# Spreading the heads' norm roots on ScalarE, and moving two pairs of value heads out of PSUM in one operation

## The chip, the cores and the metric

The kernel runs on one core of a Trainium2 chip. The metric is the device time of one execution in microseconds (us). TensorE (PE) does the matmuls; its weight loads (PEld) are listed apart. VectorE is DVE, ScalarE is ACT, GpSimd is POOL, and SyncE (SP) issues most of the transfers.

## The reference, cut to what matters

Two layers over x of 512 tokens by 1024 features. A layer is a gated feed-forward block, a token mixer with three groups of heads, and a second feed-forward block. All of it is float32. The mixer, with what the change touches:

```python
proj = h @ w_in[layer]
(qa, ka, va, qb, kb, vb, qi, ki, wi, qc, kc, vc) = jnp.split(proj, split_points, axis=-1)
oa = moba_attention(qa, ka, heads(va, N_HEADS_A))                # 4 heads, softmax
ob = dsa_attention(qb, kb, heads(vb, N_HEADS_B), qi, ki, wi)     # 4 heads, softmax over 128 chosen keys
oc = stick_breaking_attention(heads(qc, N_HEADS_C), heads(kc, N_HEADS_C), heads(vc, N_HEADS_C))  # 8 heads
o = jnp.concatenate([oa, ob, oc], axis=2)
o = (_rms(o).reshape(B, S, D_MIX) * out_g[layer].astype(jnp.float32)).astype(x.dtype)
x = x + g2 * (o @ w_out[layer])
```

Each head has 64 features. `_rms` divides each head's output, token by token, by the root of its mean square over those 64 features.

## The kernel before, in words

Activations lie with features on the 128 partitions and the 512 tokens along the row. Each float32 product is made of three matmuls of a faster format: every operand is split into a high part (a cast, on ACT) and a low part (a subtraction, on DVE), and `mm3` multiplies high by high, high by low and low by high (L323 to L325). So every piece of weights costs a transfer into one of three `raw` buffers, a cast to `whi` (L285) and a subtraction to `wlo` (L295), with five buffers for each of the two.

Work in the mixer goes by pairs of heads, eight pairs in all (0 to 3 softmax, 4 to 7 stick-breaking). The steps of all the pairs are Python generators, and a string written out by hand, `PLAN`, says which generator is advanced next. It begins

```python
ki ki ki q0 ki q0 q0 ki ki q0 ki q0 q0 c4 q0 c4 q1 q0 q1 c4 ...
```

where `ki` is the projection of the indexer's keys together with the values of pairs 4 and 5, `q0` and `q1` are projections of the indexer's queries, `c4` is the projection of queries and keys of pair 4, and the `n` steps finish a pair. The framework below it plans each engine's queue when the program is built: it takes the instructions by their place in the program, but lets one that it reckons ready go ahead of an earlier one that it reckons is still waiting. It reckons with durations of its own. It also puts all waits in. On the chip each queue then runs strictly in the planned order. Where an instruction of ACT and one of DVE read the same PSUM tile, the framework lets one wait for the other.

Values leave PSUM in `put_v`: for one tile of 128 tokens and one pair of heads (128 columns), ACT casts the columns to the high half of the tile `v` (L672) and DVE subtracts to get the low half (L673). `v_pairs` and `index_k` project the values of two pairs at once, 256 columns of one PSUM bank, and call `put_v` for one pair and then for the other. Four token tiles for each of four such groups make 32 calls in a layer. In `index_k` the evacuation of a token tile is four casts or copies on ACT (keys to `tok` at L809, indexer weights to `wi` at L810, two values at L672) and two subtractions on DVE. After the last tile, `do_rope` turns part of the keys (L651 to L654), L830 copies them, and the PE transposes them (L660) into a bank of the tag `b`, of which there are two. The first rows of the PE's queue behind that are the third tile of `q0`.

A pair is finished in `finish_pair`: ACT squares the output (L700), the PE sums the squares of each head (L706) into a bank, and `rsqrt` works out the roots on a tile of 128 partitions by 8 (4 token tiles, 2 heads). In these steps `self.logs` is true: DVE forms the argument (L337, or L341 to L343 for softmax pairs), ACT takes a logarithm and an exponential (L348, L349), and DVE makes one Newton step (L355, L356, L358). Before, the last operation of this chain also spreads each root over the 64 features of its head, by reading the small tile with a repeated index and writing 512 columns into the tile `of`: for stick-breaking pairs that is L358 itself, for softmax pairs a multiplication by the reciprocal of the softmax sum (L363). The PE then transposes the spread tile (L717), and DVE multiplies the pair's output by it (L719). There are nine finishes in a layer: seven with 512 columns and, for pair 3, two halves with 256.

Of the kernel before, what the change touches and what calls it, by code (L numbers as in the profile page):

```python
# [19 lines left out]
F32R = mybir.dt.float32r  # L20
# [3 lines left out]
ALU = mybir.AluOpType  # L24
# [3 lines left out]
P = 128  # L28
S = 512
NT = S // P  # L30
# [7 lines left out]
HD = 64  # L38
# [5 lines left out]
NIH = 8  # L44
# [141 lines left out]
class Net:  # L186
# [140 lines left out]

    def rsqrt(self, ss, shape, inv, r=None, wide=None, pin=False):  # L330

        nc = self.nc
        mk = lambda tag: self.t(self.sp, "%s%d" % (tag, int(np.prod(shape[1:]))), shape, bufs=2)
        v, y, u = mk("rv"), mk("ry"), mk("ru")
        spread = lambda t: t if wide is None else t[:, :, :, None].to_broadcast(list(wide.shape))
        if r is None:
            first = nc.vector.tensor_scalar(v, ss, inv, EPS, op0=ALU.mult, op1=ALU.add)  # L337
            if pin:
                self.tc.keep_in_program_order(first)
        else:  # L340
            nc.vector.scalar_tensor_tensor(v, ss, inv, r, op0=ALU.mult, op1=ALU.mult)  # L341
            nc.vector.tensor_mul(v, v, r)
            nc.vector.tensor_scalar(v, v, EPS, None, op0=ALU.add)  # L343
        if shape[-1] == 2 and len(shape) == 2:
            self.rsqrt_done = nc.gpsimd.tensor_tensor(y, v, self.half.to_broadcast(shape), op=ALU.pow)
            return y
        if self.logs:
            nc.scalar.activation(u, v, AF.Ln)  # L348
            nc.scalar.activation(y, u, AF.Exp, scale=-0.5)  # L349
        else:  # L350
            nc.vector.tensor_scalar(y.bitcast(I32), v.bitcast(I32), -0.5, float(0x5F3759DF),
                                    op0=ALU.mult, op1=ALU.add)
        rounds = 1 if self.logs else 3
        for i in range(rounds):
            nc.vector.tensor_mul(u, y, y)  # L355
            nc.vector.scalar_tensor_tensor(u, u, -0.5, v, op0=ALU.mult, op1=ALU.mult)  # L356
            last = i == rounds - 1 and r is None
            done = nc.vector.scalar_tensor_tensor(wide if last and wide is not None else y,  # L358
                                                  spread(u) if last else u, 1.5, spread(y) if last else y,
                                                  op0=ALU.add, op1=ALU.mult)  # L360
        self.rsqrt_done = done
        if r is not None:
            nc.vector.tensor_mul(wide, spread(y), spread(r))  # L363
        return y


# [296 lines left out]

    def new_v(self):
        return self.t(self.mp, "v", [P, NT, 2, 2, HD], F32R, bufs=4)

    def put_v(self, v, t, ps):

# [24 lines left out]
    def finish_pair(self, l, pair, cs=slice(0, S)):  # L695

        nc = self.nc
        o = self.o[pair]
        sq = self.t(self.mp, "of", [P, S], bufs=2)
        nc.scalar.activation(sq[:, cs], o[:, cs], AF.Square)  # L700
        yield
        tiles = range(cs.start // P, cs.stop // P)
        n = len(tiles)
        ss = self.bank("b", [P, n, 2])
        for i, t in enumerate(tiles):
            nc.tensor.matmul(ss[:, i, :], sq[:, t * P:(t + 1) * P], self.bones, start=True, stop=True)  # L706
        yield
        r = None
        if pair < 4:
            r = self.t(self.sp, "rs", [P, n, 2], bufs=2)  # L710
            nc.vector.reciprocal(r, self.sums[pair][:, tiles[0]:tiles[0] + n, :])
        yb = sq[:, cs].rearrange("p (t e d) -> p t e d", e=2, d=HD)
        self.rsqrt(ss, [P, n, 2], 1.0 / HD, r, yb)
        yield
        f = self.bank("b", [P, S])
        for i, t in enumerate(tiles):
            nc.tensor.transpose(f[:, t * P:(t + 1) * P], yb[:, i].rearrange("p a b -> p (a b)"), self.ident)  # L717
        yield
        nc.vector.scalar_tensor_tensor(o[:, cs], o[:, cs], self.outg[:, l, pair:pair + 1], f[:, cs],  # L719
                                       op0=ALU.mult, op1=ALU.mult)  # L720
        yield
# [80 lines left out]
    def index_k(self, l):  # L802
        nc, mp = self.nc, self.mp
        ki = self.t(mp, "tok", [P, NT, 2, HD], bufs=2)
        self.wi = self.t(mp, "wi", [P, NT, NIH], bufs=1)
        self.v.update({j: self.new_v() for j in (4, 5)})

        def evac(t, ps):
            nc.scalar.copy(ki[:, t, 0, :], ps[:, 0:HD])  # L809
            nc.scalar.copy(self.wi[:, t, :], ps[:, HD:HD + NIH])  # L810
            for i, j in enumerate((4, 5)):
                c = HD + NIH + i * P
                self.put_v(self.v[j], t, ps[:, c:c + P])

        rng = MIX_GROUPS["kiv"]
        n = sum(b - a for a, b in rng)
# [113 lines left out]
            yield from put(self.qk[4 + j], ps, scale)  # L930

    def v_pairs(self, l, grp, chunks):
        vs = {j: self.new_v() for j in chunks}
        self.v.update(vs)
        yield from self.proj_tok(l, grp, range(NT), lambda t, ps: [
            self.put_v(vs[j], t, ps[:, i * P:(i + 1) * P]) for i, j in enumerate(chunks)])

    def unit(self, pair, u):
        if pair >= 4:
# [241 lines left out]
```

## Time and profile before

| | |
|---|---|
| median of three timed runs | 2131.05 us (2129.67 to 2131.19) |
| the profiled execution: its own time | 2131.03 us |
| its span in the profile | 2129.2 us |
| PE busy | 2093.3 us (98%), 11327 matmuls |
| weight loads busy | 1803.8 us (85%) |
| DVE busy | 1276.1 us (60%) |
| ACT busy | 837.5 us (39%) |
| mean granted clock of TensorE | 0.998 |

Times inside the profile count from the start of the span. The two mixers lie at about 394 to 700 us and 1448 to 1755 us; the rest is feed-forward. A number in square brackets at the end of a timeline row is the time for which the engine sat idle before that row, and behind the arrow stands what released it as far as the profile can tell: a wait for several things is put down to the one that came last by the profile. "x4" at the end of a row means that four like instructions in a row are merged. The clock column is the share of full speed that TensorE was granted.

### The profile page before, as it was taken

How to read it: one execution, taken by the hardware profiler on the slowest of the kernel's cores; microseconds unless marked ns; L12 is line 12 of the kernel's file. 1: busy time of each engine (PE TensorE's matmuls, PEld its weight loads, DVE VectorE, ACT ScalarE, POOL GpSimd, SP SyncE). 2: the span in 40 equal slices, each digit the busy share in tenths (PEclk: the TensorE clock that was granted, in tenths of full speed). 3: DMA queues.
4: the chain of work that ended last, by engine and by line, in shares of the span. 5: the costliest groups of instructions: out<-in, count | busy, mean ns of one | idle time of the engine just before them, and what ended most of it. 6: DMA issues, size and time to landing. Idle time of an engine off the chain costs nothing.

```text
span 2129.2 us, 28611 instructions
## 1 busy us (share of the span) xinstructions
PE 2093.3 (98%) x11327; PEld 1803.8 (85%) x11327; DVE 1276.1 (60%) x2325; ACT 837.5 (39%) x1347; POOL 10.8 (1%) x24
## 2 busy tenths in 40 slices
PE   9999999999999999999999999999999999999999
PEld 6888888888998888888898888888889988888888
DVE  8773753679978677375364333346899776333332
ACT  3322222467675522222243222324766644222220
POOL 0000000000000000000000000000000000000000
PEclk9999999999999999999999999999999999999999
DMA  7883852342333388386234333324334223333331
GB/s 300 274 277 99 274 167 89 104 116 63 98 94 99 116 273 271 98 278 196 89 109 130 98 99 99 92 83 123 91 87 105 72 73 109 98 91 99 99 100 59
DMA packets 86150, 281.75 MB, mean 132 GB/s; under 512 B 10752, under 2 KB 13312, under 8 KB 86016
## 3 DMA queue, kind: packets, MB, share of 16 engines
q1 hardware_dynamic: 84576, 277.83, 42.3%
q8 instruction: 89, 1.46, 0.3%
q10 hardware_dynamic: 1440, 2.10, 0.3%
q14 instruction: 45, 0.37, 0.1%
HBM read 256.55 MB, written 2.10 MB: 121 GB/s over the span
## 4 chain that ended last, share of the span: by engine, by line
PE 81%; DVE 11%; ACT 3%; DMA 2%; issue 2%; POOL 0%; SPq 0%; POOLq 0%; DVEq 0%; ACTq 0%
PE z L323 23%; PE z L325 22%; PE z L324 22%; PE b L323 3%; PE b L325 3%; PE b L324 3%; DVE sc L881 2%; DVE m L880 2%; DVE wlo L295 2%; DVE att L594 1%; PE z L639 1%; PE z L683 1%; DMA qk<-qk 1%; DMA adaw<-in_w_ada_dram 1%; DVE tf L744 1%
## 5 line engine op out<-in xcount | busy, mean ns | idle before, releaser
L295 DVE TENSOR_TENSOR wlo<-raw,whi 128x1024 fp32r<-128x1024 f32 (+1 forms) x338 | 412.2, 1220 | 535.7 <-ACT whi L285 534.0
L285 ACT CAST whi<-raw 128x1024 fp32r<-128x1024 f32 (+1 forms) x338 | 354.9, 1050 | 842.0 <-PE z L324 772.4
L323 PE MATMUL z<-hh,whi 128*128 128x512 f32 (+1 forms) x1616 | 595.0, 369 | 3.0 <-ACT hh L454 2.3
L324 PE MATMUL z<-hl,whi 128*128 128x512 f32 (+1 forms) x1616 | 595.4, 369 | 0.3
L325 PE MATMUL z<-hh,wlo 128*128 128x512 f32 (+1 forms) x1616 | 594.5, 369 | 1.0 <-DVE wlo L295 1.0
L323 PEld LDWEIGHTS z<-hh,whi 128*128 128x128 f32 x1616 | 304.6, 189 | 55.4 <-ACT hh L454 3.9
L325 PEld LDWEIGHTS z<-hh,wlo 128*128 128x128 f32 x1616 | 304.8, 189 | 52.7 <-DVE wlo L295 2.1
L324 PEld LDWEIGHTS z<-hl,whi 128*128 128x128 f32 x1616 | 305.0, 189 | 51.5 <-DVE hl L455 1.2
L323 PE MATMUL z<-gh,whi 128*128 128x512 f32 (+1 forms) x792 | 290.9, 367 | 0.5 <-DVE xs L531 0.5
L324 PE MATMUL z<-gl,whi 128*128 128x512 f32 (+1 forms) x792 | 289.5, 366 | 0.0
L325 PE MATMUL z<-gh,wlo 128*128 128x512 f32 (+1 forms) x792 | 286.1, 366 | 0.0
L374 DVE CUSTOM_DVE_ANT_0 adaw<-adaw,silc 128x1024 f32<-128x1024 f32 x144 | 171.0, 1221 | 32.5 <-DMA adaw<-in_w_ada_dram 32.5
L323 PEld LDWEIGHTS z<-gh,whi 128*128 128x128 f32 x792 | 149.3, 188 | 28.0 <-DVE xs L531 1.2
L325 PEld LDWEIGHTS z<-gh,wlo 128*128 128x128 f32 x792 | 149.3, 189 | 24.6
L324 PEld LDWEIGHTS z<-gl,whi 128*128 128x128 f32 x792 | 149.4, 189 | 23.4
L323 PE MATMUL b<-whi,hh 128*128 128x256 f32 x544 | 156.9, 288 | 3.0 <-DVE v L673 2.1
L325 PE MATMUL b<-whi,hl 128*128 128x256 f32 x544 | 154.9, 285 | 0.0
L324 PE MATMUL b<-wlo,hh 128*128 128x256 f32 x544 | 154.8, 285 | 0.0
L531 DVE SCALAR_TENSOR_TENSOR xs<-z,mod,xs 128x512 f32<-128x512 f32 (+1 forms) x72 | 49.8, 691 | 120.8 <-PE z L325 120.8
L323 PEld LDWEIGHTS b<-whi,hh 128*128 128x128 f32 x544 | 105.1, 193 | 4.1 <-DVE osb L719 1.3
L324 PEld LDWEIGHTS b<-wlo,hh 128*128 128x128 f32 x544 | 105.0, 193 | 0.2
L325 PEld LDWEIGHTS b<-whi,hl 128*128 128x128 f32 x544 | 104.9, 193 | 0.0
(151 smaller groups left out, 2244.4 us busy)
## 6 DMA issues: line engine op xcount, KB each, us to landing
raw<-in_w_dram SPq DMA_DIRECT2D x332, 512.0 KB, 3.6
adaw<-in_w_ada_dram SPq DMA_DIRECT2D x144, 512.0 KB, 4.9
qk<-qk SPq DMA_DIRECT2D x144, 128.0 KB, 2.4
qk<-qk SPq DMA_DIRECT2D x24, 96.0 KB, 2.7
xs<-in_x_dram SPq DMA_DIRECT2D x4, 512.0 KB, 5.1
raw<-in_w_dram SPq DMA_DIRECT2D x4, 492.0 KB, 3.7
silc<-in_c_dram SPq DMA_DIRECT2D x3, 512.0 KB, 6.7
out_dram<-xs ACTq DMA_DIRECT2D x6, 256.0 KB, 2.0
```

Source lines behind the costliest of these rows:

```text
L285: nc.scalar.copy(hi[:, :n], raw[:, :n])
L295: self.nc.vector.tensor_sub(lo[:, :n], raw[:, :n], hi.bitcast(F32)[:, :n])
L323: mm(out, l[0], r[0], start=start, stop=False, **kw)
L324: mm(out, l[0], r[1], start=False, stop=False, **kw)
L325: mm(out, l[1], r[0], start=False, stop=stop, **kw)
L374: r = self.nc.vector.tensor_tensor_reduce(w, w, self.silc, 1.0, 0.0, op0=ALU.mult, op1=ALU.add, accum_out=m[:, j:j + 1])
L531: nc.vector.scalar_tensor_tensor(self.x[m][:, cs], ps[:, cs], gate[:, m:m + 1], self.x[m][:, cs], op0=ALU.mult, op1=ALU.add)
L594: nc.vector.tensor_sub(unit_sbuf(lo, u), src, unit_sbuf(hi.bitcast(F32), u))
L639: self.nc.tensor.matmul(out, a, b, start=start and i == 0, stop=stop and i == 1, skip_group_check=True)
L683: nc.tensor.matmul(outs[e][:, HT - w:], lhs, a[:, o:o + w], start=i + j == 0, stop=c == KEY_UNITS[u][-1][1] and j == 1, skip_group_check=True)
L880: nc.vector.max(m8, sc)
L881: nc.vector.match_replace(sc, m8, sc, TAKEN)
```

## The change

Two edits. The roots of a finish stay small: the last Newton step and, for softmax pairs, the multiplication by the reciprocal are done on the 128 by 8 (or 128 by 4) tile on DVE, and a copy on ACT then reads that tile with a repeated index and writes the 512 (or 256) columns of `of`. And the values of two pairs share one tile: `new_v` makes a tile of double width (two buffers instead of four, so as many bytes), and `put_v` is called once for 256 columns, so that one cast and one subtraction take the place of two of each.

```diff
-    def rsqrt(self, ss, shape, inv, r=None, wide=None, pin=False):
+    def rsqrt(self, ss, shape, inv, r=None, pin=False):
...
-        spread = lambda t: t if wide is None else t[:, :, :, None].to_broadcast(list(wide.shape))
...
-        rounds = 1 if self.logs else 3
-        for i in range(rounds):
+        for i in range(1 if self.logs else 3):
             nc.vector.tensor_mul(u, y, y)
             nc.vector.scalar_tensor_tensor(u, u, -0.5, v, op0=ALU.mult, op1=ALU.mult)
-            last = i == rounds - 1 and r is None
-            done = nc.vector.scalar_tensor_tensor(wide if last and wide is not None else y,
-                                                  spread(u) if last else u, 1.5, spread(y) if last else y,
-                                                  op0=ALU.add, op1=ALU.mult)
-        self.rsqrt_done = done
+            self.rsqrt_done = nc.vector.scalar_tensor_tensor(y, u, 1.5, y, op0=ALU.add, op1=ALU.mult)
         if r is not None:
-            nc.vector.tensor_mul(wide, spread(y), spread(r))
+            nc.vector.tensor_mul(y, y, r)
         return y
...
-    def new_v(self):
-        return self.t(self.mp, "v", [P, NT, 2, 2, HD], F32R, bufs=4)
+    def new_v(self, pairs):
+
+        v = self.t(self.mp, "v", [P, NT, 4, 2, HD], F32R, bufs=2)
+        self.v.update({j: v[:, :, 2 * i:2 * i + 2] for i, j in enumerate(pairs)})
+        return v
...
+        y = self.rsqrt(ss, [P, n, 2], 1.0 / HD, r)
         yb = sq[:, cs].rearrange("p (t e d) -> p t e d", e=2, d=HD)
-        self.rsqrt(ss, [P, n, 2], 1.0 / HD, r, yb)
+        nc.scalar.copy(yb, y[:, :, :, None].to_broadcast([P, n, 2, HD]))
...
-        self.v.update({j: self.new_v() for j in (4, 5)})
+        v = self.new_v((4, 5))
...
-            for i, j in enumerate((4, 5)):
-                c = HD + NIH + i * P
-                self.put_v(self.v[j], t, ps[:, c:c + P])
+            self.put_v(v, t, ps[:, HD + NIH:HD + NIH + 2 * P])
...
     def v_pairs(self, l, grp, chunks):
-        vs = {j: self.new_v() for j in chunks}
-        self.v.update(vs)
-        yield from self.proj_tok(l, grp, range(NT), lambda t, ps: [
-            self.put_v(vs[j], t, ps[:, i * P:(i + 1) * P]) for i, j in enumerate(chunks)])
+        v = self.new_v(chunks)
+        yield from self.proj_tok(l, grp, range(NT), lambda t, ps: self.put_v(v, t, ps[:, :2 * P]))
```

`PLAN` is the same in both kernels.

## Rows read from the trace of the kernel before

**Rows 1.** The page's first part: busy time, share of span, instructions.

```profile
PE 2093.3 (98%) x11327; PEld 1803.8 (85%) x11327; DVE 1276.1 (60%) x2325; ACT 837.5 (39%) x1347; POOL 10.8 (1%) x24
```

**Rows 2.** PE's waits over the span: total us, times, longest.

```profile
PE b L660 <- ACT v L672: 5.0, 2, 2.5
PE z L683 <- DVE att L594: 4.5, 7, 1.1
...
PE z L796 <- ACT tf L786: 2.4, 6, 0.5
...
PE b L323 <- DVE v L673: 2.1, 2, 1.0
```

**Rows 3.** Timeline of PE: start, duration, then engine, line, operation.

```profile
405.78 1.08 PE L660 MATMUL b<-rmat,tok 128*128 128x128 f32 x4 [2.44 <-ACT v L672]
...
407.30 0.41 PE L323 MATMUL b<-whi,hh 128*128 128x256 f32 x1
...
407.94 0.41 PE L323 MATMUL b<-whi,hh 128*128 128x256 f32 x1
...
409.45 0.28 PE L323 MATMUL b<-whi,hh 128*128 128x256 f32 x1
...
409.80 0.28 PE L323 MATMUL b<-whi,hh 128*128 128x256 f32 x1
```

**Rows 4.** A window behind that wait: length, busy by engine (instructions), clock, DMA.

```profile
406.00:407.00 1.00, 1.00 (x6) 1.00 (x6) 0.00 (x0) 0.10 (x1) 0.00 (x0) 0.50 0.76 291
```

**Rows 5.** Timeline of ACT ahead of that wait.

```profile
402.08 1.05 ACT L285 CAST whi<-raw 128x1024 fp32r<-128x1024 f32 x1 [1.04 <-DMA raw<-in_w_dram]
403.04 0.20 ACT L809 COPY tok<-z 128x64 f32<-128x64 f32 x1
...
404.63 0.27 ACT L672 CAST v<-z 128x128 fp32r<-128x128 f32 x1 [0.88 <-DVE v L673]
```

**Rows 6.** Timeline of DVE ahead of that wait.

```profile
399.74 0.48 DVE L673 TENSOR_TENSOR v<-z,v 128x128 fp32r<-128x128 f32 x2
400.14 1.21 DVE L295 TENSOR_TENSOR wlo<-raw,whi 128x1024 fp32r<-128x1024 f32 x1
...
403.17 1.23 DVE L295 TENSOR_TENSOR wlo<-raw,whi 128x1024 fp32r<-128x1024 f32 x1 [1.41 <-ACT whi L285]
...
404.51 0.22 DVE L651 TENSOR_TENSOR rl<-tok,late 128x64 f32<-128x64 f32 x1
```

**Rows 7.** DVE by line and shape: count, busy us, mean ns, idle before.

```profile
L692 DVE TENSOR_TENSOR osb<-osb,z 64x256 f32<-64x256 f32 x64 | 26.7, 419 | 4.4 <-ACT osb L691 2.3
...
L673 DVE TENSOR_TENSOR v<-b,v 128x128 fp32r<-128x128 f32 x48 | 13.7, 286 | 10.0 <-ACT v L672 9.8
...
L358 DVE SCALAR_TENSOR_TENSOR of<-ru,ry 128x512 f32<-128x512 f32 x8 | 5.5, 685 | 0.1
...
L363 DVE TENSOR_TENSOR of<-ry,rs 128x512 f32<-128x512 f32 x6 | 4.1, 687 | 0.1
...
L358 DVE SCALAR_TENSOR_TENSOR ry<-ru,ry 128x16 f32<-128x16 f32 x8 | 1.3, 164 | 0.0
```

**Rows 8.** ACT by line and shape, columns as above.

```profile
L672 ACT CAST v<-b 128x128 fp32r<-128x128 f32 x48 | 12.6, 263 | 21.6 <-PE b L325 11.7 <-DVE v L673 9.8
...
L905 ACT COPY tok<-b 128x256 f32<-128x256 f32 x32 | 11.8, 368 | 11.0 <-PE b L325 10.9
...
L700 ACT ACTIVATE of<-osb 128x512 f32<-128x512 f32 x14 | 8.8, 630 | 5.9 <-DVE osb L692 5.9
```

**Rows 9.** Windows, part of the first mixer, columns as in rows 4.

```profile
470.00:553.00 83.00, 78.92 (x544) 72.11 (x542) 81.81 (x188) 57.61 (x93) 0.00 (x0) 1.00 0.33 90
```

**Rows 10.** Timeline of ACT, the exponential of pair 4's finish.

```profile
492.80 0.20 ACT L349 ACTIVATE ry<-ru 128x8 f32<-128x8 f32 x1
492.90 0.91 ACT L759 ACTIVATE tf<-z 128x896 f32<-128x896 f32 x1
```

**Rows 11.** Timeline of DVE, the spread of the same finish.

```profile
494.66 0.68 DVE L358 SCALAR_TENSOR_TENSOR of<-ru,ry 128x512 f32<-128x512 f32 x1
```

## The prediction

> **What bounds the kernel now.** The first part of the page comes first: the PE is busy for 98% of the span, DVE for 60%, ACT for 39% [rows 1]. The span is 2129.2 us, so all of the PE's idle time is 36 us. Both edits only take work from DVE and ACT, or move it between them. They can help only where the PE waits for these two, and hurt only where they make a new wait. So the second view is the list of the PE's waits [rows 2]. The largest entry is the transpose of the indexer's keys (L660): 5.0 us in two waits, one in each mixer. The timeline of the PE shows the first: idle for 2.44 us, from 403.34 to 405.78 [rows 3]. The reader should see what follows it as well. Behind the wait the granted clock is 0.50 [rows 4], the lower of TensorE's two levels: three matmuls take 0.64 us start to start (407.30 to 407.94), and once the clock is back 0.35 us (409.45 to 409.80) [rows 3].
>
> The queues of ACT and DVE ahead of the wait say where it comes from [rows 5, 6]. ACT stands idle for 1.04 us for a weight transfer and casts that piece from 402.08. Only behind it come the keys of the last token tile (403.04), and the cast of that tile's second pair of values waits another 0.88 us for DVE [rows 5]. DVE subtracts that weight piece until 404.40 and gets to the rotation of the keys at 404.51; 1.27 us later the PE starts [rows 3, 6]. The profile names the last value cast as releaser, but that ended at 404.90; what the transposes read is written by the rotation and the copy at the end of DVE's chain.
>
> The third view is a window over 83 us of the mixer, from 470 to 553. DVE is busy for 81.81 of them, and the PE is idle for 4.1 [rows 9]. There DVE sets the pace, and each microsecond taken from it may come back.
>
> **The values.** 16 times a layer, two casts of 0.263 us become one of 256 columns, and two subtractions of 0.286 become one. The cast I take at 0.37 (L905, same bank, same width), the subtraction at 0.42 (L692, 256 columns from PSUM) [rows 7, 8]. That saves 0.16 us of ACT and 0.15 of DVE each time by durations. Back to back, two subtractions take 0.48 [rows 6], so DVE's queue gains only 0.06. Busy time is the small part. The larger is the alternation: cast, subtraction, cast, subtraction becomes cast, subtraction, once for each token tile.
>
> For the keys' wait I rebuild the chain. The third tile's subtraction starts at 399.74 [rows 6] and would now be whole, so PSUM is free for the fourth tile at about 400.2, not after another round trip through both engines. Its keys, weights and values then take ACT about 0.6 us, to 400.8, ahead of the weight cast that starts at 402.08. DVE is in a weight subtraction until 401.35 [rows 6], now some 0.15 later, then subtracts the values to about 401.9. The 1.27 us from the rotation to the PE contained 0.28 of the second pair's subtraction, so 1.0 remains: 402.9. The PE arrives at 403.34. The wait is gone with 0.4 us to spare, and with it the slow clock: from 405.78 to about 408.96 matmuls ran at 0.64 for 0.35, so 3.2 us held 1.75 of work and lost 1.4. One mixer gains 2.5 + 1.4 = 3.9 us, both gain 7.8.
>
> That needs the planner to order the queues so. I cannot read its order off a trace of the old kernel, so I bound it. Above: the whole 3.9. Between: the keys' copy goes ahead of the weight cast, but the subtraction that follows that cast slips in before the end of the rotation. Then DVE still sits in it until 404.40, the PE starts near 404.9, and a mixer gains 0.9, or 2.3 if a shorter wait leaves the clock up. Below: the order stays, and it gains nothing. I take the whole, since the alternation is what put the keys behind the cast.
>
> **The roots.** Per layer, seven 512-column operations of 0.685 us (L358, L363) and two of half that width go from DVE. What takes their place is of the kind of L358 on 16 columns, 0.164 us [rows 7]: about 0.52 saved in each of the seven. ACT gets a copy of 512 columns. The trace shows no copy on ACT with a repeated index. The bounds are 0.368 (half the width) and 0.630 (same width) [rows 8], and twice that if the repeated read costs extra; on DVE the spread operands show no such extra, since L358 and L363 read them at 0.69. I take 0.63. ACT is at 39%, so 2 x 5.2 us more, less 2 x 2.5 saved on the casts, is hidden beside the PE.
>
> In the window of rows 9 lie two finishes and five value evacuations: 2 x 0.52 + 5 x 0.06 = 1.3 us off DVE's queue. Bounds: 0, if what the PE waits for there is a round trip and not DVE's length, and 1.3 in each layer. I take 0.7, or 1.4 in all. The two waits for a value subtraction, 2.1 us together [rows 2], lie in that stretch too. They shrink, but DVE is late again a few instructions on, so I count them inside the 1.4.
>
> The added wait: the copy on ACT stands behind the exponential of the same finish, and its operand comes out of DVE's three or four small operations. In pair 4's finish the exponential started at 492.80, and DVE came to the last step at 494.66 [rows 10, 11]. If the planner keeps the copy right behind the exponential, ACT is held for up to 1.7 us. What stands behind it are the exponentials and casts of other pairs (here L759), and for those DVE and then the PE wait. A planner that places the copy when it reckons the operand ready avoids most of this. Bounds: 0, and another 1.2 us a layer, if the waits of L796 for ACT (2.4 us in all, rows 2) double. I take 0.3 a layer, a loss of 0.6. The transposes of a finish (L717) stand in no wait of [rows 2], so their being some 0.3 later is covered by the matmuls in front of them.
>
> No transfer and no queue of SP or POOL is moved. The double-width tile has as many bytes, and its first writer waited for both old pairs before, too.
>
> **Sum.** 2131.03 - 7.8 - 1.4 + 0.6 = 2122.4, against the profiled execution's own time of 2131.03, of which 1.8 lies outside the span; the median of the runs is 2131.05, so nothing is to be corrected. I say 2122.5.
>
> **The rivals.**
> Half of the wait stays: the order with the weight subtraction in between. For it: both queues already mix weights into other work [rows 5, 6]. Gain 0.9 to 2.3 a mixer, taken at 1.6: 2131 - 3.2 - 0.8 = 2127.
>
> The wait stays, so that the first part of the change does not do what it could: the weight cast still stands ahead of the keys, and only DVE's stretch gains: about 2130. For it: the planner reckons with its own durations, and put that cast ahead of earlier work while its transfer was 1.04 us away.
>
> Larger operations make the wait longer. In the trace the halves hardly overlap, as the 0.88 us shows [rows 5]. Were they to overlap, the first half of each merged operation would come 0.10 + 0.13 us later, over two tiles 0.5 a mixer: 2132. The Trainium skill speaks for this way (Perfetto Trace Analysis, Optimizing Scalar/DVE Operations): where ACT and DVE are not saturated but cause bubbles elsewhere, it advises to break instructions up. By that rule the sum would be 2132 and not 2122; this trace's 0.88 us of alternation speaks against it.
>
> Slower: ACT is held by the spreads. There are 18 finishes, each with up to 1.7 us of holding and 0.63 of copying. The 8.6 of gain is gone when 0.5 us of each finish reaches the PE, and the kernel is slower beyond 0.2% when 0.72 does; at 1.1 it is 2142. Against it: ACT has 25 of the 83 us free even in DVE's full stretch [rows 9], and only L796 is seen waiting for softmax's exponentials.
>
> **How the numbers follow.** Whole wait gone 0.45, half 0.22, wait stays 0.20, longer by merging 0.03, slower by the spreads 0.10. The prediction is the first. With all the upper bounds it gains 2 x (3.9 + 1.3) plus some of the other waits, 2117.5; the third case reaches 2131. So the range is 2117.5 to 2131, leaving out the last two cases and the edges. The likeliest case alone spans 2119 to 2125. What a measurement here can tell from no change is about 0.2%, or 4.3 us, so faster means below 2126.8: all of the first case and a good part of the second, 0.62. Within 0.2%: 0.28. Slower: 0.10.
>
> **What would show it.** In the trace of the changed kernel, the wait of L660 gone from the PE's waits and the clock at 1.00 there; on ACT, the last tile's L809 ahead of the cast that waits for its transfer; a merged cast near 0.37, a merged subtraction near 0.42; DVE some 13 us less busy and ACT some 5 us more; the spread copy near 0.63 with little idle time ahead of it. The prediction is wrong if L660 still waits over 1 us, if the time saved comes back as a longer wait for the transfers of `qk` soon after, or if PE's waits for ACT grow by more than 2 us a layer.

## The result, and the profile after

The changed kernel takes 2118.49 us, the median of six runs (2117.37 to 2120.59); the kernel before, run beside it, 2130.7 us (2127.51 to 2131.35). The ratio is 0.9945, with a 95% interval of 0.9935 to 0.9956: 12.2 us less, where 8.5 were forecast. The profiled execution took 2117.8 us with a span of 2115.9, against 2131.03 and 2129.2 before; these two are 13.2 us apart, a little more than the medians. Of the runs reported below, one of experiment 4 took 6952.47 us in place of 2122 to 2125, and its median leaves that one out.

The page's first part, against [rows 1]:

```profile
PE 2087.0 (99%) x11327; PEld 1801.0 (85%) x11327; DVE 1265.3 (60%) x2293; ACT 844.1 (40%) x1333; POOL 10.7 (1%) x24
```

DVE is busy 10.8 us less and ACT 6.6 more (13 and 5 were forecast). Neither is worth 12 us by itself. The PE's waits of the changed kernel, against [rows 2] (total us, times, longest; the line numbers have moved: L654 was L660, L680 was L683, L794 was L796):

```profile
PE z L680 <- DVE att L588: 4.6, 6, 1.3
PE z L730 <- ACT att L587: 3.5, 2, 1.7
...
PE z L633 <- DMA qk<-qk: 2.2, 2, 1.2
...
PE b L323 <- DVE v L670: 0.9, 2, 0.5
...
PE z L794 <- ACT tf L784: 0.3, 2, 0.2
```

The wait for the keys, 5.0 us before, is not in the list at all. The wait for the values' subtraction has fallen from 2.1 to 0.9, and the wait for the softmax exponentials from 2.4 to 0.3. The second row is a wait that was shorter before.

The queues of ACT and DVE where the keys' wait was, against [rows 5, 6]. ACT first:

```profile
400.08 0.22 ACT L807 COPY tok<-z 128x64 f32<-128x64 f32 x1
400.19 0.18 ACT L808 COPY wi<-z 128x8 f32<-128x8 f32 x1
400.24 0.40 ACT L669 CAST v<-z 128x256 fp32r<-128x256 f32 x1
401.51 1.05 ACT L285 CAST whi<-raw 128x1024 fp32r<-128x1024 f32 x1 [0.87 <-DMA raw<-in_w_dram]
```

Then DVE:

```profile
400.82 0.41 DVE L670 TENSOR_TENSOR v<-z,v 128x256 fp32r<-128x256 f32 x1
401.16 0.21 DVE L645 TENSOR_TENSOR rl<-tok,late 128x64 f32<-128x64 f32 x1
...
401.87 0.29 DVE L826 COPY tok<-tok 128x256 f32<-128x256 f32 x1
402.60 1.23 DVE L295 TENSOR_TENSOR wlo<-raw,whi 128x1024 fp32r<-128x1024 f32 x1 [0.44 <-ACT whi L285]
```

The last tile's keys, weights and values now stand ahead of the weight cast that waits for its transfer, and the rotation ahead of the long weight subtraction. DVE's copy of the keys ends at 402.16, and the PE's transposes start at 402.49, without a wait:

```profile
402.49 0.60 PE L654 MATMUL b<-rmat,tok 128*128 128x128 f32 x4
```

Windows over the stretch that [rows 4] looks into, over the second mixer's, and over the two stretches of softmax units (length, busy by engine with instructions, granted clock, DMA share, GB/s):

```profile
394.00:420.00 26.00, 25.35 (x164) 22.90 (x163) 15.85 (x34) 11.69 (x25) 0.00 (x0) 1.00 0.59 167
1445.00:1475.00 30.00, 29.35 (x192) 26.44 (x191) 16.17 (x32) 12.71 (x25) 0.00 (x0) 1.00 0.58 165
...
640.00:700.00 60.00, 59.47 (x427) 54.84 (x426) 47.97 (x121) 34.44 (x79) 0.69 (x1) 1.00 0.39 115
1690.00:1750.00 60.00, 59.56 (x429) 55.10 (x428) 47.97 (x119) 34.21 (x77) 0.69 (x1) 1.00 0.32 90
```

The clock is 1.00 throughout the first two.

Where the time came from can be read by comparing the start of the n-th matmul in both traces (us from the start of the span; the last column is after minus before):

```
n       before     after     difference
0          1.34      1.34      0.00    first matmul
1680     377.65    376.98     -0.67    before the first mixer
2000     430.57    425.44     -5.13    behind the transposes of the keys
2200     466.97    461.16     -5.81    behind a wait for qk
2560     525.24    521.18     -4.07    in DVE's full stretch
3500     650.52    646.40     -4.11
3780     692.58    686.83     -5.75    behind the softmax units
7500    1450.74   1444.75     -5.99    second mixer, before the keys
7600    1469.44   1459.48     -9.96    behind the transposes of the keys
8300    1584.81   1574.81     -9.99    in DVE's full stretch
9000    1675.83   1665.88     -9.95
9420    1740.50   1728.60    -11.90    behind the softmax units
9720    1781.19   1767.95    -13.24    behind a half clock of before
11300   2122.73   2109.42    -13.31    end
```

The keys' wait gave 4.5 and 4.0 us, with its slow clock and what came late behind it. The softmax units gave 1.6 and 2.0. DVE's full stretch gave nothing on balance: in the first mixer 1.7 us were lost there, in the second nothing either way. A half clock (a short stretch at a granted clock of 0.50) that stands near 1774 us in this execution of before, and not in the one of after, gave 1.3.

The loss has its place. DVE and ACT there, then the PE, then a window behind it:

```profile
512.29 0.41 DVE L877 MATCH_REPLACE8 sc<-m,sc 128x256 f32<-128x256 f32 x1
512.73 0.43 DVE L876 MAX8 m<-sc 128x8 f32<-128x256 f32 x1
513.08 1.07 DVE L742 SCALAR_TENSOR_TENSOR tf<-z,tf 128x896 f32<-128x896 f32 x1
```

```profile
511.31 0.96 ACT L740 ACTIVATE tf<-tf 128x896 f32<-128x896 f32 x1
...
514.18 0.94 ACT L587 CAST att<-tf 128x896 fp32r<-128x896 f32 x1 [1.37 <-DVE tf L742]
```

```profile
515.17 1.31 PE L730 MATMUL z<-att,rmat 128*128 128x512 f32 x6 [1.74 <-ACT att L587]
```

```profile
515.00:520.00 5.00, 4.83 (x23) 4.55 (x24) 4.89 (x11) 1.57 (x5) 0.00 (x0) 0.66 0.00 0
```

ACT's logarithm (L740) is done at 512.27, but DVE comes to the sum that needs it at 513.08, behind two instructions of the indexer's top-k. The PE waits 1.74 us for the cast of that sum, and the clock falls: 1.4 of the 1.7 us are this half clock. In the second mixer the same wait lasts 1.75 us, and the clock stays at 1.00. The place before, logarithm, sum and PE:

```profile
517.25 0.95 ACT L742 ACTIVATE tf<-tf 128x896 f32<-128x896 f32 x1
```

```profile
518.43 1.08 DVE L744 SCALAR_TENSOR_TENSOR tf<-z,tf 128x896 f32<-128x896 f32 x1
```

```profile
520.53 2.42 PE L732 MATMUL z<-att,rmat 128*128 128x512 f32 x12 [0.83 <-ACT att L593]
```

The sum stood 0.23 us behind the end of the logarithm, and stands 0.81 behind it now; that is 0.58 of the 0.91 us by which the wait has grown. The other 0.34 is the PE's: it comes 1.16 us behind the end of the logarithm, and came 1.50 behind it before, since its wait for the values, about 4 us earlier, has fallen from 1.05 to 0.46 us.

### The profile page after: what moved, and what is told of

It reads as the page before. It is cut to its first block, busy times and chain, and to the rows that moved or that the text cites. A ratio compares the mean times of both kernels' runs of the same rounds, so it can differ in the third digit from the quotient of the medians.

```text
span 2115.9 us, 28552 instructions
## 1 busy us (share of the span) xinstructions
PE 2087.0 (99%) x11327; PEld 1801.0 (85%) x11327; DVE 1265.3 (60%) x2293; ACT 844.1 (40%) x1333; POOL 10.7 (1%) x24
## 4 chain that ended last, share of the span: by engine, by line
PE 85%; DVE 10%; issue 2%; ACT 1%; DMA 1%; POOL 0%; POOLq 0%; DVEq 0%; ACTq 0%; SPq 0%
PE z L323 23%; PE z L325 23%; PE z L324 23%; PE b L323 4%; PE b L325 3%; PE b L324 3%; DVE sc L877 2%; PE z L633 2%; DVE m L876 2%; DVE att L588 2%; DVE wlo L295 1%; PE z L680 1%; PE z L794 1%; DVE tf L742 1%; PE z L730 1%
```

## The experiments

The change has three parts that can be made apart: the values merged where they come with the keys, the values merged in the other three projections, and the roots on ACT. Six of the twelve runs, with the kernel before and the changed one, fill the table of all combinations at the end of this section; the other six try a mechanism.

**The keys' projection, and all values.** Experiment 1 merges the values everywhere and leaves the roots as before:

```diff
         if pair < 4:
...
-        y = self.rsqrt(ss, [P, n, 2], 1.0 / HD, r)
         yb = sq[:, cs].rearrange("p (t e d) -> p t e d", e=2, d=HD)
-        nc.scalar.copy(yb, y[:, :, :, None].to_broadcast([P, n, 2, HD]))
+        self.rsqrt(ss, [P, n, 2], 1.0 / HD, r, yb)
```

(as an edit to the changed kernel, with the old `rsqrt`). Expected: 

> The kernel before with the values of two pairs moved in one operation everywhere, and the roots spread on VectorE as before. Theory (the keys' wait is the gain): L660's wait and the slow clock behind it are gone in both mixers, 2 x 3.9 us, so 7.8 to 8.5 us faster than before, near 2122.5; the softmax stretch (620 to 700 us) keeps its waits of 1.2 us for the exponentials. Rival (the roots on ScalarE carry half of the gain): only 5 to 6 us faster. Rival (every part counts by its busy time): under 3 us.

Measured: 2126.18 us, ratio 0.9978 (0.9970 to 0.9987). The keys' wait is gone, but the wait for the split of a stick-breaking unit (L735, L732 before) has grown from 1.7 us to 4.3.

Experiment 2 is the other half, the roots alone: the values as before, and the two lines above as in the changed kernel. Expected: 

> The kernel before with the roots kept small and spread by ScalarE, and the values as before. Theory as predicted: L660's wait stays at about 2.5 us in each mixer with the half clock behind it, the full stretch of VectorE gives 0 to 1 us a mixer, ScalarE's holding costs 0.3: 2129 to 2131. Rival, from the traces of the two kernels: the waits of PE for the exponentials (1.2 us a mixer) go, and the softmax stretch gives 1.6 to 1.9 us a mixer: 2126 to 2127.5. Rival (ScalarE held): slower, 2132 or more.

Measured: 2129.2 us, ratio 0.9994 (0.9986 to 1.0003). Its waits of the PE (L654 is the keys' transposes, L791 the softmax units' transposes):

```profile
PE b L654 <- ACT v L666: 4.9, 2, 2.5
PE z L633 <- DMA qk<-qk: 4.4, 4, 1.4
PE b L323 <- DVE v L667: 3.7, 2, 1.8
...
PE z L791 <- ACT tf L781: 0.4, 2, 0.2
```

The keys' wait is untouched. The wait for the exponentials is gone here as in the changed kernel (2.4 before, [rows 2]), so the roots alone are enough for it. They are not the only way to it: in experiments 1 and 10, where the roots stay on DVE and the other values are merged, this wait is 0.7. In its place the waits for the values' subtraction and for transfers of `qk` have grown, 2.1 to 3.7 and 3.7 to 4.4.

Experiment 3 merges only in the projection with the keys:

```diff
     def v_pairs(self, l, grp, chunks):
-        v = self.new_v(chunks)
-        yield from self.proj_tok(l, grp, range(NT), lambda t, ps: self.put_v(v, t, ps[:, :2 * P]))
+        self.new_v(chunks)
+        yield from self.proj_tok(l, grp, range(NT), lambda t, ps: [
+            self.put_v(self.v[j], t, ps[:, i * P:(i + 1) * P]) for i, j in enumerate(chunks)])
```

Expected: 

> The kernel before with one cast and one subtraction for 256 columns in the keys' projection alone (4 of the 16 evacuations of a layer); the other three projections of values use two of each as before. Theory: nearly all that the merging of values gives comes from here: 7.8 us faster, near 2123, and L660 in no wait. Rival (all evacuations count alike): a quarter of what merging everywhere gives.

Measured: 2123.73 us, ratio 0.9970 (0.9959 to 0.9981). The keys' wait is gone and the other waits are close to what they were.

Experiment 4 merges nothing. In the kernel before, the keys and weights of both token tiles of a PSUM tile are copied ahead of their four value casts:

```diff
-            for i in range(2):
-                evac(2 * hf + i, z[:, 512 * i:])
+            for put in (keys, evac):
+                for i in range(2):
+                    put(2 * hf + i, z[:, 512 * i:])
```

Expected: 

> The kernel before with nothing merged: in the keys' projection the keys and weights of both token tiles of a PSUM tile are copied first, and the four casts and subtractions of values follow. As many instructions as before, of the same sizes. Theory (the wait came from the place of the last keys behind the alternation of casts and subtractions, and so behind a weight cast that waits for its transfer): L660's wait goes, 7 to 8 us faster, near 2123. Rival (it was the number and length of the evacuating operations): no change, 2130 to 2131.

Measured: 2122.41 us, ratio 0.9967 (0.9954 to 0.9980), which can't be told from experiment 3. Its ACT queue:

```profile
398.32 0.21 ACT L809 COPY tok<-z 128x64 f32<-128x64 f32 x1 [0.58 <-PE z L325]
398.43 0.17 ACT L810 COPY wi<-z 128x8 f32<-128x8 f32 x1
398.49 0.23 ACT L809 COPY tok<-z 128x64 f32<-128x64 f32 x1
398.59 0.30 ACT L672 CAST v<-z 128x128 fp32r<-128x128 f32 x1
...
401.76 1.05 ACT L285 CAST whi<-raw 128x1024 fp32r<-128x1024 f32 x1 [0.60 <-DMA raw<-in_w_dram]
402.71 0.26 ACT L672 CAST v<-z 128x128 fp32r<-128x128 f32 x1
```

A value cast still stands behind the weight cast, and the PE does not mind. So the order alone is enough to make the wait and to mend it: the keys stood behind the alternation of casts and subtractions, and so behind the weight cast. Fewer instructions were one way to mend it.

**The half clock.** Experiment 5 is the kernel before with extra matmuls in the wait:

```diff
         ps = self.bank("b", [P, S])
+        for i in range(pads):
+            self.tc.keep_in_program_order(self.nc.tensor.matmul(
+                ps, self.h[0][0][:, :P], self.h[0][0], start=True, stop=True))
```

with ten of them ahead of the keys' transposes, and none elsewhere. Expected: 

> The kernel before with ten extra matmuls of 128x512 on TensorE just ahead of the transposes of the keys in each mixer, written into the bank that the transposes then overwrite; the order on every other engine is as before, and the transposes still wait for the last copy of the keys. Theory (half of what the removed wait gave back is the clock): the transposes come no earlier, but TensorE is busy through the 2.4 us, the windows behind them (near 406 and 1460 us) show a granted clock of 1.00 in place of 0.50, and 2 x 1.4 = 2.8 us go: about 2127.7. Rival (the slow stretch costs nothing because VectorE is late there anyway): 2130.5, the same as before, whatever the clock shows.

Measured: 2127.4 us, ratio 0.9987 (0.9978 to 0.9996): 2.4 us less, for more work. The two waits, filled:

```profile
1455.85 2.49 PE L660 MATMUL b<-hh 128*128 128x512 f32 x10
1458.50 0.66 PE L663 MATMUL b<-rmat,tok 128*128 128x128 f32 x4
```

```profile
406.00:407.00 1.00, 1.00 (x10) 1.00 (x9) 0.13 (x1) 0.59 (x1) 0.00 (x0) 1.00 0.86 299
1448.00:1475.00 27.00, 26.37 (x168) 23.68 (x167) 15.50 (x36) 11.49 (x29) 0.00 (x0) 1.00 0.54 157
```

The granted clock is 1.00 where it was 0.50 [rows 4]. The waits' length, some 5 us, is still paid; the 2.4 us are the clock's share of what the keys' wait cost.

That share is not due every time. Experiment 2 keeps the keys' wait, as experiments 6 and 10 below do (experiment 10 merges the other values alone). In the profiled executions of experiments 2 and 10 the clock stayed at 1.00 behind the first mixer's wait (2.39 and 2.36 us) and fell behind the second's (2.54 and 2.62); in those of experiment 6 and of the kernel before it fell behind both. The windows of experiment 10:

```profile
404.00:409.00 5.00, 4.06 (x32) 3.96 (x33) 2.38 (x6) 2.22 (x5) 0.00 (x0) 1.00 0.41 125
1458.00:1464.00 6.00, 5.30 (x31) 5.25 (x32) 1.93 (x5) 1.96 (x4) 0.00 (x0) 0.72 0.32 92
```

**Undoing one part of the changed kernel.** Experiment 6 splits the values again in the keys' projection alone:

```diff
-            self.put_v(v, t, ps[:, HD + NIH:HD + NIH + 2 * P])
+            for i, j in enumerate((4, 5)):
+                c = HD + NIH + i * P
+                self.put_v(self.v[j], t, ps[:, c:c + P])
```

Expected: 

> The changed kernel with one part undone: in the projection with the indexer's keys the two pairs' values leave PSUM in two casts and two subtractions for a tile of tokens again; roots on ScalarE and merged values in the other three projections stay. Theory (the order on the bank makes the wait, whatever else is changed): the transposes of the keys wait 2 x 2.5 us again with their half clock, 7 to 8 us slower than the changed kernel, about 2126. Rival (the rest of the change has moved ScalarE and VectorE far enough ahead that the keys are no longer late): 2118.5 to 2120, no wait at the transposes.

Measured: 2128.88 us, ratio 0.9997 (0.9989 to 1.0006). Nearly the whole gain is gone, 10.4 us by the medians. The order is back too: the weight cast ahead of the keys, and the last value cast behind the 0.88 us of alternation, as in [rows 5]:

```profile
401.44 1.05 ACT L285 CAST whi<-raw 128x1024 fp32r<-128x1024 f32 x1 [1.09 <-DMA raw<-in_w_dram]
402.40 0.20 ACT L807 COPY tok<-z 128x64 f32<-128x64 f32 x1
...
403.99 0.27 ACT L669 CAST v<-z 128x128 fp32r<-128x128 f32 x1 [0.88 <-DVE v L670]
```

```profile
405.14 0.63 PE L654 MATMUL b<-rmat,tok 128*128 128x128 f32 x4 [2.49 <-ACT v L669]
```

Set beside the changed kernel matmul by matmul, it loses 4.1 us at the first mixer's keys and 3.7 at the second's; a half clock near 1573 us costs 1.6 more, and the one of the changed kernel near 516 us, which is not there, gives 1.4 back.

Experiment 7 copies the keys first in the changed kernel, as experiment 4 does in the kernel before. Expected: 

> The changed kernel, with the keys and weights of both tiles of a PSUM tile copied ahead of their merged values. Theory: the wait of the transposes is gone already, so earlier keys give nothing: 2118.5, within 1 us. Rival: merged values come later by two copies and the queues of ScalarE and VectorE are ordered otherwise behind them, so that a wait elsewhere comes or goes: 2114 or 2122.

Measured: 2120.64 us, ratio 0.9960 (0.9946 to 0.9973), which can't be told from the changed kernel. The earlier keys give nothing more.

Experiment 8 splits the values again in the other three projections alone, by the diff of experiment 3. Expected: 

> The changed kernel with the other part undone: in the three other projections of values the pairs leave PSUM in two casts and two subtractions; the keys' projection stays merged and the roots stay on ScalarE. If the parts added up (keys alone -6.7, roots alone -1.3): about 2122.5, and merging the other three projections is worth the 4 us that are left. Rival (merging the others gives nothing, and the 4 us come of the roots and the keys together, once the softmax stretch has no other late thing): 2118.5.

Measured: 2119.82 us, ratio 0.9957 (0.9944 to 0.9969). The run does not tell the two apart: its interval holds both what the parts give together, 0.9970 x 0.9994 = 0.9964, and the changed kernel's 0.9945. Its waits show the wait for the values' subtraction at 3.7 us, as in experiment 2, where the changed kernel has 0.9, and hardly any of the one that is longer in the changed kernel:

```profile
PE b L323 <- DVE v L670: 3.7, 2, 1.8
...
PE z L730 <- ACT att L587: 0.4, 1, 0.4
```

**What took the gain in DVE's full stretch.** Experiment 9 gives the planner one edge in each mixer: a top-k instruction may not stand ahead of the sum of the late unit (`self.late` collects the sums of L742 in order):

```diff
-            nc.vector.match_replace(sc, m8, sc, TAKEN)
+            hold = self.tc.issue_after(self.late[7].ins) if (t, i) == (1, 12) else ExitStack()
+            with hold:
+                nc.vector.match_replace(sc, m8, sc, TAKEN)
```

Expected: 

> The changed kernel with one edge for the planner in each mixer: the replacement of the thirteenth round of the smallest top-k group may not stand ahead of the softplus sum of the unit whose split TensorE waits 1.74 us for. Theory (the time that the merged subtraction freed on VectorE was filled by the planner with two top-k instructions of 0.41 and 0.43 us ahead of that sum): the wait falls from 1.74 to about 0.9 us in each mixer, 2 x 0.8 = 1.6 us less, and 1.4 us more in the executions in which the half clock followed it: 2115.5 to 2117. Rival (the chain before it, exponential and logarithm on ScalarE, is the limit, or the top-k instructions are missed as much later on): 2118.5, or a new wait and up to 2121.

Measured: 2120.57 us, ratio 0.9955 (0.9941 to 0.9968). The place answers to the theory in part (ACT, DVE, PE):

```profile
512.29 0.96 ACT L740 ACTIVATE tf<-tf 128x896 f32<-128x896 f32 x1
```

```profile
513.28 1.09 DVE L742 SCALAR_TENSOR_TENSOR tf<-z,tf 128x896 f32<-128x896 f32 x1
```

```profile
515.40 1.20 PE L730 MATMUL z<-att,rmat 128*128 128x512 f32 x6 [1.23 <-ACT att L587]
```

The sum now starts 0.03 us behind ACT's logarithm, and the wait is 1.23 us in place of 1.74, in the second mixer 1.22 in place of 1.75. No half clock stands behind it (the window from 510 to 520 us has 1.00), but that is no proof that the edge took it away: in the first mixers of experiments 6, 7 and 12, as profiled, the wait is 1.74 to 1.75 us and the clock is 1.00 behind it too. The wait does not fall to 0.9, because ACT's own chain is now what is late: the rival's limit. By the medians nothing is gained, so this version does not beat the changed kernel. Two half clocks, near 715 and 1765 us, stand in its profiled run and not in that of the changed kernel.

Experiment 10 merges the values in the three other projections alone (the edit of experiment 6 made to experiment 1). Expected: 

> The kernel before with merged values in the three projections that hold values alone; the projection with the indexer's keys and the roots are as before. If the parts added up (values everywhere -4.3, keys' projection alone -6.7): +2.4, about 2132.5, with the transposes of the keys waiting 2 x 2.5 us as before. Rival (fewer instructions on two engines are worth what they took off the waits for the values' banks, 1.2 us between [rows 2] and the same wait after): 2129.

Measured: 2132.18 us, ratio 1.0007 (0.9998 to 1.0016). The wait for the values' subtraction has fallen from 2.1 us [rows 2] to 0.4, but that for the split of a stick-breaking unit, 1.7 us in the trace of before, has grown to this:

```profile
PE z L735 <- ACT att L593: 4.3, 2, 2.2
```

For the first mixer the queues say what it is made of. The sum stands 0.56 us behind the end of the logarithm (515.57 and 515.01), behind one top-k replacement, where it stood 0.23 behind before: 0.33 of the 1.33 us by which the wait has grown. The other 1.0 is the PE, which comes 0.51 us behind the logarithm in place of 1.50; its wait for the values just ahead has fallen from 1.05 us to 0.20.

**The spread.** Experiment 11 does each spread twice in the changed kernel:

```diff
-        nc.scalar.copy(yb, y[:, :, :, None].to_broadcast([P, n, 2, HD]))
+        for _ in range(2):
+            nc.scalar.copy(yb, y[:, :, :, None].to_broadcast([P, n, 2, HD]))
```

Expected: 

> The changed kernel with every spread of the roots on ScalarE done twice, 18 copies of 0.62 us more (0.3 where a half is finished); order on VectorE as in the changed kernel. Theory (ScalarE has idle time where the spreads stand, and what waits for them is not on the path): no more than 0.5 us, about 2118.5 to 2119. Rival (each spread holds ScalarE ahead of work that TensorE waits for, the prediction's 0.3 us a layer or its bound of 1.2): 2119.1 to 2121.

Measured: 2122.63 us, ratio 0.9965 (0.9953 to 0.9978). ACT by line and shape (count, busy us, mean ns, idle before):

```profile
L712 ACT COPY of<-ry 128x512 f32<-128x512 f32 x28 | 17.4, 620 | 6.0 <-DVE ry L357 4.4 <-DVE ry L355 1.0
```

By the medians that is 4 us more than the changed kernel, with intervals that just meet. The matmul by matmul comparison says where: 0.7 us in the first part of the execution, 0.7 and 0.6 in the stretches from 425 to 461 and 1476 to 1513 us, and 1.5 by a half clock near 1767, all of them places without a spread; and in the stretches that hold the finishes, 489 to 690 and 1538 to 1740 us, 0.4 each. So as many spreads again cost the PE 0.4 us a layer, close to the prediction's 0.3 and far from its bound of 1.2. This prices the copying and not the holding: the second copy of a pair has its operand already and waits for nothing, so ACT's idle time ahead of the spreads is 8.8 us in all, and 8.3 in the changed kernel. What stands in the other places is taken to be of the kind by which executions differ.

**A filler in the wrong place.** Experiment 12 was to fill a wait before the second feed-forward part of a layer with four matmuls:

```diff
+            elif f == 1:
+                for i in range(4):
+                    self.tc.keep_in_program_order(self.nc.tensor.matmul(
+                        pss[0], self.identr, self.rmat.rearrange("p a b -> p (a b)"), start=True, stop=True))
```

Expected: 

> The changed kernel with four extra matmuls of 128x512 on TensorE ahead of the first product of the second feed-forward part in each layer, where it waits 0.99 us for the first normed chunk after a wait of 0.51 us; they go to a bank that the product then overwrites, and every other engine's order is as in the changed kernel. In this place (near 715 and 1766 us) the half clock stood in the profiled runs of five of the experiments, and not in that of the changed kernel. Theory (the executions of one kernel differ by the number of half-clock stretches of 1.4 us, and this place is where they come and go): the mean clock stays at 0.999 or above in nearly all executions, the median falls by 0.5 to 1.5 us to about 2117.5, and the runs lie within 2 us. Rival (the stretches come from elsewhere, or the idle before the matmuls is enough): 2118.5 to 2120.5, runs from 2117 to 2122, clocks of 0.998 among them.

Measured: 2121.24 us, ratio 0.9960 (0.9946 to 0.9973). The extra matmuls ran here,

```profile
698.93 1.09 PE L483 MATMUL z<-rmat 128*128 128x512 f32 x4
```

ahead of the first half of the tokens. The wait that they were meant for stands ahead of the second half, 15 us later, and was not filled; the clock fell there (a mean of 0.66 from 713 to 718 us). So the run says nothing on its question. Set beside the changed kernel matmul by matmul, the extra matmuls, 0.93 us of work in each mixer, cost 0.13 us each time, because the changed kernel stands still there for most of that time; its weight loads wait for the normed tokens:

```profile
699.88 0.30 PEld L323 LDWEIGHTS z<-hh,whi 128*128 128x128 f32 x2 [0.34 <-ACT hh L448]
```

The half clocks behind the unfilled waits cost 1.2 us near 716 and 1.5 near 1766. That they come and go shows in the changed kernel, which has the same wait of 0.99 us at both places at a clock of 1.00.

**All combinations**, as ratios to the kernel before (half an interval is about 0.0010):

| keys' values | other values | roots on DVE | roots on ACT |
|---|---|---|---|
| split | split | 1 | 0.9994 |
| split | merged | 1.0007 | 0.9997 |
| merged | split | 0.9970 | 0.9957 |
| merged | merged | 0.9978 | 0.9945 |

Down the columns: merging the keys' values is worth 0.0029 to 0.0052, 6 to 11 us, in each of the four pairs. Merging the others makes no difference that is clear of the intervals: +0.0007 and +0.0008 with the roots on DVE, +0.0003 and -0.0012 with the roots on ACT. The roots on ACT are worth 0.0006 to 0.0013, within the intervals too, except once both others are merged: 0.0033. The parts do not add up: alone they give 0.9970 x 1.0007 x 0.9994 = 0.9971, together 0.9945.

Much of that goes with the clock. A half clock lowers the mean clock of an execution by 0.0008 (the profiled execution of experiment 7 has none and a mean of 1.000, that of experiment 2 has five and 0.996), and costs about 1.4 us. Averaged over the runs the mean clock is 0.9990 in the changed kernel, 0.9980 in experiment 3, 0.9975 to 0.9980 in the kernel before, and 0.9968 and 0.9971 in experiments 2 and 10. An estimate from these figures: the changed kernel has 1.2 half clocks an execution, the kernel before about 3, experiment 3 2.5, and experiments 2 and 10 about 4. By that, 3 to 4 us of the 5.5 by which the whole exceeds its parts are half clocks.

## Why the prediction was right, and where it was not

**The first wait.** This step was right in mechanism and size: 7.8 us predicted, 8.4 measured by the matmuls (4.46 and 3.97), and by the medians 6.7 in experiment 3 and 8.0 in experiment 4. The order on both queues is the one rebuilt in the prediction. The mixer starts 0.7 us earlier than before; counted from there, ACT is done with the last tile 0.5 later than rebuilt, and DVE's copy of the keys ends at what was 402.8, where 402.9 was worked out for the PE's start. Of the four cases that the prediction bounded, the whole came. The split into waiting and clock, 2 x 2.5 and 2 x 1.4, holds for the executions in which the half clocks stand: with the clock kept up and the wait left, experiment 5 gains 2.4 of the 2.8. That they stand was taken from one trace; in six of the eight such waits that were profiled they do.

**The rival that larger operations lengthen the wait.** For the keys' wait it fell, in every kernel that merges there. The rule of the Trainium skill (Perfetto Trace Analysis, Optimizing Scalar/DVE Operations), to break instructions up where an engine that is not saturated causes bubbles elsewhere, points the wrong way at this place: with larger instructions the 5.0 us of bubble went, and experiment 4 shows that the order and not the size mattered. In experiment 10 the PE's wait for a split grew from 1.7 us to 4.3 with merged values, but there the rule's condition is not met, since DVE is busy for 81.98 of the 83 us from 467 to 550 there; and in the first mixer most of that growth is the PE coming earlier.

**DVE's full stretch.** This is the step that failed: 1.4 us of gain predicted, 1.7 lost. Of the loss, 1.4 is one half clock, which the same wait has in some executions and not in others; without it the stretch lost 0.3 us in the first mixer and nothing in the second, where 0.7 of gain was taken for each. The durations were right (merged subtractions of 0.42, as taken from L692, and casts of 0.37), and so is the remark on the waits for the values: they fell from 2.1 to 0.9, and "DVE is late again a few instructions on", where the wait for the split grew from 1.7 to 3.5. What failed is the sentence that each microsecond taken from DVE "may come back"; it assumed that DVE's queue keeps its order. Two top-k instructions of 0.41 and 0.43 us stand ahead of the sum now, and stood behind it before. Experiment 9 shows what that is worth: with these behind the sum, the wait falls by 0.5 us. The other 0.4 by which the wait is longer than the 0.8 of before is ACT's chain, which is late for a PE that no longer waits as long for the values. That the planner moved the top-k there because merging had freed the time is argued, not shown.

**The roots.** The duration was right: the copy with a repeated index takes 0.62 us for 512 columns, where 0.63 was taken. ACT is held, too; its own list of waits has the spread:

```profile
ACT of L711 <- DVE ry L357: 7.1, 8, 1.2
ACT of L711 <- DVE ry L355: 1.0, 2, 0.6
```

8.1 us in ten waits. The error was in what it costs: 0.6 us of loss predicted, and 3.6 gained by the matmuls in the softmax units. There the prediction feared that the waits of L796 for ACT's exponentials would double; they fell from 2.4 to 0.3, and experiment 2 shows that the roots alone do this (0.4). Merging the other values alone brings them to 0.7, but by the matmuls experiment 10 then loses 0.7 us in the first softmax units and gains 0.7 in the second, since a wait of 1.0 us for `qk` takes the place in the first. DVE's work in the two 60 us windows is 47.97 us each, where it was 49.34 and 51.47 before; that the exponentials come earlier because DVE's share of a finish does is argued, not shown. The rival "ACT is held by the spreads" fell, but not for lack of a price: experiment 11 finds 0.4 us a layer for as much copying again. No run prices the holding by itself.

**The sum.** The forecast of 2122.5 us was 4 us too high, and that it came so near is in part luck: two terms of small size had the wrong sign, and their errors nearly cancel: -1.4 became about +1.7, +0.6 became -3.6. The rest of the 13.3 us by the matmuls is outside the terms: 0.7 before the first mixer, 0.7 from a shorter wait for `qk` in the first (3.7 to 2.2 in all), 0.2 between the mixers, and 1.3 from the half clock that stands in the profiled run of before near its end.

**What stays open.** Why the whole is worth more than its parts is settled only as far as the waits and the mean clocks above go. Nor is it settled why the same wait is followed by a half clock in one execution and not in another, and so why the changed kernel has fewer of them.

## What to carry to other kernels

Where an engine waits for a small result that two other engines pass to and fro, look first at what stands ahead of it in their queues: here the keys could be had by merging or simply by copying them first, for the same 7 to 8 us. When a planner orders the queues, time taken from a full engine is not yet gained; look at what the planner puts there, and at what then comes late. Make the parts of a change one by one and also undo them one by one: here the part that was worth 11 us in the whole was worth 6 alone, and the roots, which alone could not be told from nothing, were worth 7 once both others were merged.

## What the runs showed of the hardware

A wait can cost more than its length: behind 2.44 us of idle time TensorE's granted clock fell to 0.50, the lower of its two levels, for a price of 1.4 us. Ten matmuls into a bank that was about to be overwritten cost nothing in that wait (the transposes behind it started at 405.56 us, before at 405.78) and kept the clock at 1.00.

The price is not due every time. In the fourteen profiled executions a half clock followed six of the eight waits of 2.4 to 2.6 us for the keys (the kernel before and experiments 2, 6 and 10), and three of the ten waits of 1.74 to 1.75 us for the split (the changed kernel and experiments 6, 7, 11 and 12). A wait of 0.51 and one of 0.99 close together, before the second feed-forward part, were followed by one in at least one mixer in ten of the fourteen, 15 of the 28 times. Much of the spread between executions of one kernel goes with this: of the runs of experiment 5, those with a mean clock of 1.000 took 2124.8 to 2126.3 us, and those with 0.998 took 2127.4 to 2130.5.

On ACT, a copy that reads each element 64 times by a repeated index takes 0.62 us for 512 columns, no longer than the square of 512 plain ones at 0.63 [rows 8].
